# 48 tokens of the last-but-one gathered tile moved behind the last u rows, and the left-hand SBUF buffers set 32 bytes lower, in a GLA/GatedDeltaNet/PEER layer

## The chip, the cores and the metric

The kernel runs on one core of one Trainium2 chip. The metric is the device time of one execution in microseconds (us). The kernel before takes 3274.96 us, the median of three runs between 3272.29 and 3275.75 us.

## What is computed

One layer for 1,024 new frames and 32 sample frames of width 1,024: a mixer of two recurrent heads, then PEER, then a norm. The change lies in PEER, which gives every frame 128 experts (8 heads with 16 each) out of 16,384:

```
act = gelu(einsum('thkd,td->thk', peer_u[eidx], x))
out = einsum('thk,thkd->td', gate * act, peer_v[eidx])
x = x + out ; y = rms_norm(x) * norm_final_w
```

## The kernel before

The frames lie in tiles of 128 tokens, 0 to 7, and "S" with the 32 sample frames. Two ways are used for PEER.

**Dense tiles** (2, 3, 4, 5). All 16,384 experts are computed, in 128 blocks of 128 experts. `activations(blk)` loads a block of u as `ux` (512 KB), splits it into a rounded part and a rest (`uh`, `ul`), and makes `pD` with 24 matmuls of 128x512: 8 slices of the width, each three times (`mm3`: `hh` with `uh`, `hh` with `ul`, `hl` with `uh`; lines 197 to 199). ScalarE makes the Gelu (`w`), VectorE multiplies with the gates `G`, and `w` is split into `wh`, `wl`. The block of v (`vx`, 512 KB) becomes `vh`, `vl`. Four blocks together give `pV` (8 groups of 12 matmuls of 128x512), which VectorE adds to `acc` (L1039). In such a matmul the first operand after the arrow of a row (`hh`, `hl`, `vh`, `vl`) streams through the array, and the second (`uh`, `ul`, `wh`, `wl`) is loaded as its weights. At the end `final_norm` scales each `acc` (L1052) and it is stored.

**Gathered tiles** (0, 1, S, 6, 7, in this order). `u_phase` gathers for each of 128 slots one row of u per token (`ug`, 128x1024, 512 KB, an indirect DMA that GpSimd issues, L1098), and VectorE multiplies and sums it with the token (L1099). `v_phase` gathers for each of 128 tokens its 128 rows of v (L1133); after four tokens TensorE multiplies them with the weights `wd` (eight matmuls of 32x512, L1139, called a round here; 32 rounds for a tile), and the next tokens follow. At the tile's end `pv` is added to the residual `xf`, which is normed and stored; `xf`, the norm's junk and the norm's weights take three of the five `vg` buffers.

`v_phase(t, more)` has five buffers `vg`. With `more` it may also take the four buffers `ug` of the u rows (three in one pool, one in another): token i then uses buffer i mod 9. Up to this version `more` is True for the last tile alone. A tile's v phase is woven with the u phase of the next tile, one gather of each in turn, and the v side is issued at high priority. A scheduler orders the instructions of each engine by its own timing model when the kernel is built; on the chip each engine runs its list in that order.

The order is written out at the end of the kernel: `dense(late)` first, then the loop over the gathered tiles. The scheduler mixes the two, so that TensorE has dense matmuls between the rounds.

SBUF is filled from two sides. On the left lie, among others, the constants (`ident`, `iota128`, `offs`, `firsts`, `noffs`), `c1` to `c3` (later `acc`), the projection's `hh`, `hl`, `wh`, `wl`, and in the dense part `ux`, `vx`, `uh`, `ul`, `G`. On the right lie the dense part's `hh`, `hl`, `w`, `wh`, `wl`, `vh`, `vl`, and `ug`, `vg`, `wd`.

Of the kernel before, what the change touches and what calls it, by code (L numbers as in the profile page):

```python
# [11 lines left out]
F32 = mybir.dt.float32  # L12
# [3 lines left out]
U16 = mybir.dt.uint16  # L16
BF16 = mybir.dt.bfloat16
AF = mybir.ActivationFunctionType
ALU = mybir.AluOpType
AX = mybir.AxisListType  # L20

P = 128
# [10 lines left out]
OFFS = [0, 16, 24, 29, 33, 36, 38, 40, 42, 43, 44, 45, 46, 47, 48, 49]  # L33

PROJ = [[0, 1, "S"], [2, 3, 4], [5, 6, 7]]
GROUPS = [[0], [1, "S"], [2, 3], [4, 5], [6, 7]]

DENSE = [2, 3, 4, 5]
# [20 lines left out]
VB = 5  # L59
NG = NT + 1 - len(DENSE)  # L60
WDB = 3
EARLY = [0, 1, "S"]

SP0 = 2
# [5 lines left out]
def bc(ap, shape):  # L70
    return ap.to_broadcast(shape)
# [3 lines left out]
def layer_kernel(ctx: ExitStack, tc: tile.TileContext, A: dict):  # L75
    nc = tc.nc
    mm = nc.tensor.matmul

    const = ctx.enter_context(tc.tile_pool(name="const", bufs=1))
# [20 lines left out]
    def mixer_tables():  # L100

        tc.keep_in_program_order(nc.scalar.preload_act_table_set("natural_log_exp_and_others"))
# [18 lines left out]
    nc.gpsimd.iota(iota128, pattern=[[1, P]], base=0, channel_multiplier=0,  # L121
                   allow_small_or_imprecise_dtypes=True)

    offs = const.tile([P, 15], F32, name="offs")
    for q in range(15):
        nc.gpsimd.memset(offs[:, q:q + 1], float(OFFS[q + 1]))
    firsts = const.tile([P, 16], U16, name="firsts")
    for q in range(16):
        nc.gpsimd.memset(firsts[:, q:q + 1], OFFS[q] * P)

    noffs = const.tile([P, 15], F32, name="noffs")
    nc.vector.tensor_scalar(noffs, offs, -1.0, 1.0, op0=ALU.mult, op1=ALU.add)

    def row_bcast(name, src, n, pool):
        t = pool.tile([P, n], F32, name=name)
# [3 lines left out]
    def ntok(t):  # L139
        return DEC if t == "S" else P  # L140
# [913 lines left out]
    def idx_of(ap):  # L1054
        return bass.IndirectOffsetOnAxis(ap=ap, axis=0)
# [28 lines left out]
    def u_phase(t, ei, eiT, gate):  # L1084

        act = gs.tile([P, P], F32, name="act", bufs=2)
        h2 = ge.tile([P, D], F32, name="h2", bufs=1)
        slots = DEC if t == "S" else P
        if t == "S":
            for c in range(4):  # L1090
                nc.sync.dma_start(h2[c * DEC:(c + 1) * DEC], h2d[t])
        else:
            nc.sync.dma_start(h2, h2d[t])
        yield None
        for k in range(slots):
            e = t == 0 or k % 4 < 3
            g = (ge if e else gp).tile([P, D], F32, name="ug", bufs=UB if e else 1)
            nc.gpsimd.indirect_dma_start(out=g, out_offset=None, in_=A["u"], in_offset=idx_of(ei[:, k:k + 1]))  # L1098
            nc.vector.scalar_tensor_tensor(g, g, 1.0, h2, op0=ALU.mult, op1=ALU.mult,  # L1099
                                           accum_out=act[:, k:k + 1])  # L1100
            yield None
        with tc.high_priority():
            nc.scalar.activation(act[:, :slots], act[:, :slots], AF.Gelu_apprx_tanh)
            if t in EARLY:
                mixer_tables()
            nc.vector.tensor_tensor(act[:, :slots], act[:, :slots], gate[:, :slots], op=ALU.mult)
            wT = gs.tile([P, P], F32, name="wT", bufs=2)
            pw = bank("pw", "pv")
            by_slot(pw, act, t)
            nc.scalar.copy(wT[:, :ntok(t)], pw[:, :ntok(t)])  # L1110
        ready[t] = eiT, wT

    def v_phase(t, more):

        eiT, wT = ready[t]
        pv = [bank("pv0", "pv"), bank("pv1", "pv")]

        ns = ntok(t) // 4
        W4 = wT[:, :ntok(t)].rearrange("p (c r) -> p c r", c=4)
        for r in range(ns):  # L1120
            wd = gp.tile([P, 4, 32], F32, name="wd", bufs=WDB)
            nc.vector.scalar_tensor_tensor(wd, bc(iota128[:, None, :32], [P, 4, 32]), float(r),
                                           bc(W4[:, :, r:r + 1], [P, 4, 32]), op0=ALU.is_equal, op1=ALU.mult)
            vs = []
            for c in range(4):
                tok = c * ns + r

                own = (r * 4 + c) % (VB + UB + 1)
                if more and own >= VB:
                    g = (ge if own < VB + UB else gp).tile([P, D], F32, name="ug", bufs=UB if own < VB + UB else 1)  # L1130
                else:
                    g = gp.tile([P, D], F32, name="vg", bufs=VB)
                nc.gpsimd.indirect_dma_start(out=g, out_offset=None, in_=A["v"],  # L1133
                                             in_offset=idx_of(eiT[:, tok:tok + 1]))
                vs.append(g)
                yield None

            def product(half, c):
                return mm(pv[half][c * 32:(c + 1) * 32, :], wd[:, c, :], vs[c][:, half * 512:(half + 1) * 512],  # L1139
                          start=(r == 0), stop=(r == ns - 1), tile_position=(0, c * 32), skip_group_check=True)  # L1140

            with tc.issue_after(product(0, 3).ins):
                for half in range(2):
                    for c in range(3 + half):
                        product(half, c)
        x = gp.tile([P, D], F32, name="xf", tag="vg", bufs=VB)
        if t == "S":
            nc.gpsimd.memset(x, 0.0)
            for c in range(4):
                nc.sync.dma_start(x[c * 32:c * 32 + ns], xdram[t][c * ns:(c + 1) * ns])  # L1150
        else:
            nc.sync.dma_start(x, xdram[t])
        for half in range(2):
            cs = slice(half * 512, (half + 1) * 512)
            nc.vector.tensor_tensor(x[:, cs], x[:, cs], pv[half], op=ALU.add)
        nf = gp.tile([P, D], F32, name="nf", tag="vg", bufs=VB)
        load_nfin(nf)
        final_norm(x, gp, nf)
        if t == "S":
            for c in range(4):  # L1160
                nc.sync.dma_start(A["ys"][c * ns:(c + 1) * ns], x[c * 32:c * 32 + ns])
        else:
            nc.sync.dma_start(A["yp"][t * P:(t + 1) * P, :], x)
# [8 lines left out]
    def some(gen, n, pace=1):  # L1172

        while n is None or n > 0:
            for _ in range(pace):
                if next(gen, 0) == 0:
                    return
            n = n and n - 1
            yield None

    def values(t, more):
        return urgent(v_phase(t, more))

    def weave(*gens):
        gens = [g for g in gens if g is not None]
        while gens:
            for g in list(gens):
                if next(g, 0) == 0:
                    gens.remove(g)
# [44 lines left out]
    sel, picked, mixT = {}, {}, {}  # L1234
# [54 lines left out]
    gctx.close()  # L1289
    dv = ctx.enter_context(tc.tile_pool(name="dv", bufs=1, side="right", reuse_waits="tile"))  # L1290
    dense(late)
    prev = None
    for t in [t for g in GROUPS for t in g if t not in DENSE]:
        weave(values(prev, False) if prev is not None else None, u_phase(t, *sel[t]))
        prev = t
    weave(values(prev, True))


OUTS = dict(yp=(SEQ, D), ys=(DEC, D), o_gla_p=(4, 64, 128), o_gdn_p=(4, 128, 128), o_conv_p=(128, 12, 3),
# [62 lines left out]
```

## Time and profile before

| | |
|---|---|
| median of three runs | 3274.96 us (3272.29 to 3275.75) |
| the profiled execution: its own time | 3281.99 us |
| its span, first to last instruction | 3280.3 us |
| TensorE (PE) busy | 3064.6 us, 93% of the span |
| VectorE, GpSimd, ScalarE busy | 2291.9, 1316.8, 1282.0 us |
| moved by DMA | 959.04 MB, mean 292 GB/s |
| mean granted clock of TensorE | 0.961 |

The profile is of one execution. A view by stretches gives each engine's busy time between two times; a timeline lists instructions with what ended the idle time before them. Matmuls are pipelined: one row's duration is longer than the distance between two starts, and the distance is what a matmul costs.

### The profile page before, as it was taken

The page shows a single profiled execution, that of the slowest core. Times are in us where ns is not written, and L with a number is a line of the kernel's source. Part 1 is how long each engine was busy: PE and PEld are TensorE (multiplying, and loading weights), DVE is VectorE, ACT ScalarE, POOL GpSimd, SP SyncE. Part 2 cuts the span into 40 slices and gives each one's busy share as a digit, 9 for nine tenths or more (in the row PEclk, how much of TensorE's full clock was granted, in tenths as well). Part 3 has the DMA queues.
Part 4 walks back from the last instruction along what each step waited for, and adds up shares of the span by engine and source line. Part 5 has one row for each costly group of instructions (what it writes and reads, how often), then busy time and mean ns, then how long its engine had stood idle before and what let it go on. Part 6 is the DMA issues. An engine that isn't in the chain of part 4 may idle for free.

```text
span 3280.3 us, 49506 instructions
## 1 busy us (share of the span) xinstructions
PE 3064.6 (93%) x17739; PEld 2451.9 (75%) x17739; DVE 2291.9 (70%) x5692; ACT 1282.0 (39%) x2748; POOL 1316.8 (40%) x1181
## 2 busy tenths in 40 slices
PE   6999997799999999889789999999999999999997
PEld 6889986689878877767567777777777777776664
DVE  4457478888878989899977767766766767434332
ACT  6758434544332226787523222223222222223111
POOL 2100004433244544433355545544555555233454
PEclk9989998799999989899799999999999999999998
DMA  5532468888788889999999889889998898777988
GB/s 155 167 108 90 155 195 299 271 296 294 272 309 317 310 322 348 314 345 334 328 351 333 336 319 363 329 324 356 334 337 346 300 366 312 281 258 258 339 320 301
DMA packets 363977, 959.04 MB, mean 292 GB/s; under 512 B 35746, under 2 KB 137523, under 8 KB 359635
## 3 DMA queue, kind: packets, MB, share of 16 engines
q0 software_dynamic: 156672, 570.49, 47.5%
q1 hardware_dynamic: 141266, 351.84, 30.5%
q10 hardware_dynamic: 65792, 33.56, 3.5%
q8 instruction: 139, 2.28, 0.3%
q14 instruction: 108, 0.88, 0.1%
HBM read 893.00 MB, written 62.76 MB: 291 GB/s over the span
## 4 chain that ended last, share of the span: by engine, by line
PE 47%; DMA 1%; issue 1%; DVE 1%; POOL 0%; ACT 0%; POOLq 0%; DVEq 0%; ACTq 0%
PE pD L198 7%; PE pD L197 7%; PE pD L199 7%; PE pV L197 7%; PE pV L199 7%; PE pV L198 7%; PE pv L1139 6%; DMA vg<-v,eiT 1%; DMA ug<-u,ei 0%; POOL ug L1098 0%; DVE ug L1099 0%; DVE c L887 0%; DVE vl L192 0%; POOL ug L1133 0%; DVE xf L1052 0%
## 5 line engine op out<-in xcount | busy, mean ns | idle before, releaser
L1098 POOL DMA_INDIRECT ug<-u,ei x544 | 647.2, 1190 | 1148.8 <-DVE ug L1099 514.0
L1133 POOL DMA_INDIRECT vg<-v,eiT x488 | 582.9, 1194 | 625.8 <-PE pv L1139 453.2
L1099 DVE SCALAR_TENSOR_TENSOR ug<-ug,h 128x1024 f32<-128x1024 f32 x544 | 659.9, 1220 | 106.4 <-DMA ug<-u,ei 104.0
L197 PE MATMUL pD<-hh,uh 128*128 128x512 f32 x1024 | 408.6, 399 | 4.3 <-ACT uh L191 4.2
L198 PE MATMUL pD<-hh,ul 128*128 128x512 f32 x1024 | 408.6, 399 | 3.3 <-DVE ul L192 3.3
L199 PE MATMUL pD<-hl,uh 128*128 128x512 f32 x1024 | 407.4, 398 | 0.0
L198 PE MATMUL pV<-vh,wl 128*128 128x512 f32 x1024 | 401.4, 393 | 0.0
L199 PE MATMUL pV<-vl,wh 128*128 128x512 f32 x1024 | 400.0, 393 | 0.0
L197 PE MATMUL pV<-vh,wh 128*128 128x512 f32 x1024 | 381.5, 395 | 5.0 <-DVE acc L1039 4.3
L1039 DVE TENSOR_TENSOR acc<-acc,pV 128x512 f32<-128x512 f32 x248 | 164.0, 684 | 239.1 <-PE pV L199 213.0
L191 ACT CAST vh<-vx 128x1024 fp32r<-128x1024 f32 x128 | 129.2, 1047 | 509.9 <-PE pV L198 420.0
L991 ACT ACTIVATE w<-pD 128x512 f32<-128x512 f32 x128 | 76.5, 598 | 541.0 <-PE pD L199 482.3
L1139 PE MATMUL pv<-vg,wd 128*32 128x512 f32 x1952 | 267.6, 619 | 17.2 <-DMA vg<-v,eiT 16.4
L192 DVE TENSOR_TENSOR wl<-w,wh 128x512 fp32r<-128x512 f32 x302 | 207.3, 688 | 100.5 <-ACT wh L191 70.3
L191 ACT CAST wh<-w 128x512 fp32r<-128x512 f32 x302 | 186.0, 619 | 185.1 <-PE pcm L324 61.7
L534 PE MATMUL pq<-h2T,wqb 128*128 128x256 f32 (+2 forms) x1280 | 249.0, 348 | 3.5 <-ACT sc L556 2.0
L197 PEld LDWEIGHTS pD<-hh,uh 128*128 128x128 f32 x1024 | 193.4, 189 | 65.6 <-issue 14.1
L197 PEld LDWEIGHTS pV<-vh,wh 128*128 128x128 f32 x1024 | 192.3, 188 | 66.9 <-issue 14.2
L198 PEld LDWEIGHTS pD<-hh,ul 128*128 128x128 f32 x1024 | 193.3, 189 | 64.9 <-issue 12.2
L199 PEld LDWEIGHTS pD<-hl,uh 128*128 128x128 f32 x1024 | 193.2, 189 | 56.7 <-issue 11.7
L199 PEld LDWEIGHTS pV<-vl,wh 128*128 128x128 f32 x1024 | 192.7, 188 | 55.1 <-issue 14.3
L534 PEld LDWEIGHTS pq<-h2T,wqb 128*128 128x128 f32 x1280 | 211.2, 194 | 25.9 <-issue 3.0
(334 smaller groups left out, 5457.9 us busy)
## 6 DMA issues: line engine op xcount, KB each, us to landing
ux<-ut SPq DMA_DIRECT2D x128, 512.0 KB
vx<-v SPq DMA_DIRECT2D x128, 512.0 KB
wqb<-wq SPq DMA_DIRECT2D x80, 576.0 KB
gd<-gst ACTq DMA_DIRECT2D x16, 2048.0 KB
G<-gd SPq DMA_DIRECT2D x32, 1024.0 KB
w<-win_c SPq DMA_DIRECT2D x96, 256.0 KB
wch<-wout SPq DMA_DIRECT2D x40, 512.0 KB
w<-win_t SPq DMA_DIRECT2D x72, 256.0 KB
```

What stands on the lines that cost most here:

```text
L191: nc.scalar.copy(hi, x)
L192: nc.vector.tensor_tensor(lo, x, hi.bitcast(F32), op=ALU.subtract)
L197: mm(out, a[0], b[0], start=first, stop=False, **kw)
L198: mm(out, a[1], b[0], start=False, stop=False, **kw)
L199: mm(out, a[0], b[1], start=False, stop=last, **kw)
L534: mm(p[:, :N], w[:, kb, :], h2T[:, kb, :], start=(kb == 0), stop=(kb == KB - 1))
L991: nc.scalar.activation(w, pD, AF.Gelu_apprx_tanh)
L1039: nc.vector.tensor_tensor(acc[ti][:, cs], before[:, cs], p, op=ALU.add)
L1098: nc.gpsimd.indirect_dma_start(out=g, out_offset=None, in_=A["u"], in_offset=idx_of(ei[:, k:k + 1]))
L1099: nc.vector.scalar_tensor_tensor(g, g, 1.0, h2, op0=ALU.mult, op1=ALU.mult, accum_out=act[:, k:k + 1])
L1133: nc.gpsimd.indirect_dma_start(out=g, out_offset=None, in_=A["v"], in_offset=idx_of(eiT[:, tok:tok + 1]))
L1139: return mm(pv[half][c * 32:(c + 1) * 32, :], wd[:, c, :], vs[c][:, half * 512:(half + 1) * 512], start=(r == 0), stop=(r == ns - 1), tile ...
```

## The change

The weave of the last tile's u phase with tile 6's v phase takes only 80 of tile 6's 128 tokens (`SHARE`). Then `more` is set to True, a list that `v_phase` reads token by token, and the other 48 tokens of tile 6 follow, with all nine buffers. Then comes tile 7's v phase as before. Separately, `offs` is dropped, `noffs` is written directly, and `firsts` has 64 bytes where it had 32.

```diff
+SHARE = 80
-    offs = const.tile([P, 15], F32, name="offs")
-    for q in range(15):
-        nc.gpsimd.memset(offs[:, q:q + 1], float(OFFS[q + 1]))
-    firsts = const.tile([P, 16], U16, name="firsts")
+    firsts = const.tile([P, 32], U16, name="firsts")[:, :16]
     noffs = const.tile([P, 15], F32, name="noffs")
-    nc.vector.tensor_scalar(noffs, offs, -1.0, 1.0, op0=ALU.mult, op1=ALU.add)
+    for q in range(15):
+        nc.gpsimd.memset(noffs[:, q:q + 1], float(1 - OFFS[q + 1]))
...
-                if more and own >= VB:
+                if more[0] and own >= VB:
...
-    prev = None
-    for t in [t for g in GROUPS for t in g if t not in DENSE]:
-        weave(values(prev, False) if prev is not None else None, u_phase(t, *sel[t]))
-        prev = t
-    weave(values(prev, True))
+    gathered, more, sums = [t for g in GROUPS for t in g if t not in DENSE], [False], None
+    for t in gathered:
+
+        weave(some(sums, SHARE) if sums and t == gathered[-1] else sums, u_phase(t, *sel[t]))
+        if t == gathered[-1]:
+            more[0] = True
+            weave(sums)
+        sums = values(t, more)
+    weave(sums)
```

**Where buffers lie.** From `noffs` on, every buffer on the left starts 32 bytes lower in its partition; the right side stays. First bytes, and their remainders by 512 (a matmul's operands start at multiples of 512 bytes from there):

| matmul | streamed operand | weights, before | weights, after |
|---|---|---|---|
| `pD` | `hh` 150304 (288), `hl` 133920 (288) | `uh` 51008 (320), `ul` 59200 (320) | `uh` 50976 (288), `ul` 59168 (288) |
| `pV` | `vh` 100960 (96), `vl` 117344 (96) | `wh` 84576 (96), `wl` 92768 (96) | the same |
| `pcm` (projection) | `hh` 155616 (480) | `wh` 181856 (96) | `hh` and `wh` both 32 lower (448, 64) |

**Order on GpSimd** (`ug<-u` is a u row, `vg<-v` and `ug<-v` are v rows in a v buffer or in a u buffer). The list of the kernel before from tile 7's last u rows on:

```order
L1098 DMA ug<-u,ei 128x1024 x3
L1133 DMA ug<-v,eiT 128x1024
L1133 DMA vg<-v,eiT 128x1024 x4
L1133 DMA ug<-v,eiT 128x1024 x3
L1133 DMA vg<-v,eiT 128x1024 x65
L1133 DMA ug<-v,eiT 128x1024 x4
L1133 DMA vg<-v,eiT 128x1024 x5
```

The same place with the change (its line numbers are one lower):

```order
L1097 DMA ug<-u,ei 128x1024 x3
L1132 DMA ug<-v,eiT 128x1024
L1132 DMA vg<-v,eiT 128x1024 x4
L1132 DMA ug<-v,eiT 128x1024 x3
L1132 DMA vg<-v,eiT 128x1024 x12
L1132 DMA ug<-v,eiT 128x1024
L1132 DMA vg<-v,eiT 128x1024 x5
L1132 DMA ug<-v,eiT 128x1024 x4
L1132 DMA vg<-v,eiT 128x1024 x5
```

Before, the first four v rows in u buffers belong to tile 7, and 65 v rows in the five `vg` follow; now the four belong to tile 6, and its last 48 tokens alternate between both kinds, as tile 7's did and do. The u rows stand where they stood.

**Order on TensorE**, the end of the list before (`pv_28049` and `pv_28050` are the two halves of `pv`):

```order
L199 MATMUL pV<-vl,wh 128x512
L1139 MATMUL pv_28049<-vg,wd 32x512
L1139 MATMUL pv_28049<-ug,wd 32x512
L1139 MATMUL pv_28049<-vg,wd 32x512 x2
L1139 MATMUL pv_28050<-ug,wd 32x512
L1139 MATMUL pv_28050<-vg,wd 32x512 x3
L1139 MATMUL pv_28049<-ug,wd 32x512
L1139 MATMUL pv_28049<-vg,wd 32x512 x2
L1139 MATMUL pv_28049<-ug,wd 32x512
L1139 MATMUL pv_28050<-vg,wd 32x512 x2
L1139 MATMUL pv_28050<-ug,wd 32x512 x2
```

The last round with the change, and what follows it:

```order
L1138 MATMUL pv_28047<-vg,wd 32x512
L1138 MATMUL pv_28047<-ug,wd 32x512 x2
L1138 MATMUL pv_28047<-vg,wd 32x512
L1138 MATMUL pv_28048<-ug,wd 32x512 x2
L1138 MATMUL pv_28048<-vg,wd 32x512 x2
L196 MATMUL pD<-hh,uh 128x512
L197 MATMUL pD<-hh,ul 128x512
L198 MATMUL pD<-hl,uh 128x512
```

Before, three rounds stand last with nothing between them (the third is left out here); now 113 dense matmuls stand behind the last round, 21 of `pD` and 92 of `pV`. From tile 6's 21st round on both lists hold 44 rounds and 1,391 dense matmuls. Between the last round of tile 6 and the first of tile 7 stand 55 dense matmuls before and 92 now; between tile 6's 20th and 21st round 47 before and 40 now, and its 22nd follows the 21st at once.

**Order on ScalarE** with the change, near its end (the norm of tile 7's `xf`, then the last Gelu):

```order
L190 CAST wh<-w 128x512
L166 ACTIVATE rs_junk,rs_ss<-xf 128x1024
L171 ACT_TABLE_LOAD
L171 ACTIVATE rs_r<-rs_ss,eps 128x1
L172 ACT_TABLE_LOAD
L172 ACTIVATE rs_r<-rs_r 128x1
L990 ACT_TABLE_LOAD
L990 ACTIVATE w<-pD 128x512
L104 ACT_TABLE_LOAD
L190 CAST wh<-w 128x512
```

Before, the last Gelu had one table load behind it and none ahead, and that norm stood at the list's end.

## Rows read from the trace of the kernel before

**Rows 1.** The page: span, and busy time of each engine.

```profile
span 3280.3 us, 49506 instructions
PE 3064.6 (93%) x17739; PEld 2451.9 (75%) x17739; DVE 2291.9 (70%) x5692; ACT 1282.0 (39%) x2748; POOL 1316.8 (40%) x1181
```

**Rows 2.** By stretches: length, busy us (instructions) of PE, PEld, DVE, ACT, POOL; clock, DMA, GB/s.

```profile
2900.00:3000.00 100.00, 100.00 (x489) 71.62 (x482) 41.28 (x54) 24.42 (x32) 29.39 (x29) 1.00 0.73 258
3000.00:3100.00 100.00, 98.19 (x494) 66.02 (x493) 40.69 (x57) 28.10 (x37) 41.20 (x42) 1.00 0.85 310
3100.00:3150.00 50.00, 50.00 (x261) 32.71 (x260) 18.99 (x27) 10.15 (x13) 24.10 (x24) 1.00 0.89 334
3250.00:3281.00 31.00, 11.91 (x64) 3.21 (x56) 4.93 (x6) 3.29 (x8) 7.05 (x7) 0.69 0.61 230
```

**Rows 3.** Timeline of PE, its last rows (start, us; idle before and its releaser).

```profile
3252.46 0.40 PE L199 MATMUL pV<-vl,wh 128*128 128x512 f32 x1
...
3260.16 1.03 PE L1139 MATMUL pv<-ug,wd 128*32 128x512 f32 x1 [4.82 <-DMA ug<-v,eiT]
...
3269.09 1.03 PE L1139 MATMUL pv<-vg,wd 128*32 128x512 f32 x1 [5.29 <-DMA vg<-v,eiT]
...
3271.67 0.90 PE L1139 MATMUL pv<-vg,wd 128*32 128x512 f32 x1
```

**Rows 4.** By stretches, within the last rounds.

```profile
3260.00:3265.00 5.00, 3.64 (x16) 0.68 (x16) 0.00 (x0) 0.00 (x0) 0.00 (x0) 0.50 1.01 385
```

**Rows 5.** Timeline of PE around tile 6's last rounds and tile 7's first.

```profile
2855.05 1.92 PE L1139 MATMUL pv<-vg,wd 128*32 128x512 f32 x16
...
3023.84 0.40 PE L197 MATMUL pD<-hh,uh 128*128 128x512 f32 x1
3026.05 1.07 PE L1139 MATMUL pv<-vg,wd 128*32 128x512 f32 x8 [1.81 <-DMA vg<-v,eiT]
```

**Rows 6.** Timeline of GpSimd: issues of v rows around those rounds.

```profile
2848.21 0.94 POOL L1133 DMA_INDIRECT vg<-v,eiT  x1 [0.31 <-issue]
...
3017.86 1.67 POOL L1133 DMA_INDIRECT vg<-v,eiT  x1 [2.98 <-DVE xf L1052]
...
3021.84 0.97 POOL L1133 DMA_INDIRECT vg<-v,eiT  x1 [2.31 <-DMA yp<-xf]
```

**Rows 7.** Timeline of DVE at the end: the last dense sum, its norm, tile 7's norm.

```profile
3252.89 0.69 DVE L1039 TENSOR_TENSOR acc<-acc,pV 128x512 f32<-128x512 f32 x1 [1.66 <-PE pV L199]
3255.36 1.28 DVE L1052 SCALAR_TENSOR_TENSOR acc<-acc,rs_r,nfD 128x1024 f32<-128x1024 f32 x1 [1.78 <-ACT rs_r L173]
...
3275.12 1.29 DVE L1052 SCALAR_TENSOR_TENSOR xf<-xf,rs_r,nf 128x1024 f32<-128x1024 f32 x1 [1.78 <-ACT rs_r L173]
```

**Rows 8.** Groups of ScalarE from 1600 us on: table loads (count, busy us, mean ns).

```profile
L991 ACT ACT_TABLE_LOAD x6 | 7.7, 1283 | 0.1
```

**Rows 9.** Timeline of PE: first and last of 34 `pD`, of 23 `pV` back to back.

```profile
3003.92 0.39 PE L198 MATMUL pV<-vh,wl 128*128 128x512 f32 x1
...
3008.91 0.39 PE L199 MATMUL pV<-vl,wh 128*128 128x512 f32 x1
...
3016.14 0.39 PE L197 MATMUL pD<-hh,uh 128*128 128x512 f32 x1
```

**Rows 10.** Timeline of PE in the projection: 20 `pcm` of 384 columns between these.

```profile
248.82 0.87 PE L324 MATMUL pcm<-hl,wh 128*128 128x384 f32 x4
...
252.34 0.33 PE L754 MATMUL pi<-T,XT 128*128 128x64 f32 x2
```

**Rows 11.** Groups of PE: count, busy us, mean ns, idle before.

```profile
L199 PE MATMUL pD<-hl,uh 128*128 128x512 f32 x1024 | 407.4, 398 | 0.0
L199 PE MATMUL pV<-vl,wh 128*128 128x512 f32 x1024 | 400.0, 393 | 0.0
```

**Rows 12.** Groups of DVE from 1600 us on, the same columns.

```profile
L192 DVE TENSOR_TENSOR ul<-ux,uh 128x1024 fp32r<-128x1024 f32 x128 | 156.6, 1224 | 16.0 <-ACT uh L191 14.3 <-issue 1.5
L192 DVE TENSOR_TENSOR vl<-vx,vh 128x1024 fp32r<-128x1024 f32 x128 | 154.3, 1219 | 37.4 <-ACT vh L191 28.6 <-issue 8.8
```

## The prediction

> **What bounds the kernel now.** I read the page first: PE is busy for 93% of the span and no other engine comes near [rows 1]. A mean over stages decides nothing, so the view by stretches came next. From about 1800 us on PE is busy practically all the time at the full clock, up to 3250 us: 100 of 100, 98.2 of 100, 50 of 50 us. Only in the last 31 us is it busy for 11.9 [rows 2]. So TensorE bounds the stage in which the change lies, and the reader should see what follows: gathering rows faster is worth nothing there by itself. It pays only where PE waits for a row.
>
> The timeline shows these places. The last dense matmul starts at 3252.46. Then PE waits 4.82 us for a v row, works, waits 5.29 us for another, and its last row begins at 3271.67 [rows 3]. [...] A second wait, of 1.81 us, lies between tile 6 and tile 7 at 3026.05 [rows 5].
>
> Why the rows are late shows on GpSimd. With five buffers four rows are in flight per round: the last row for the round that starts at 2855.05 is issued at 2848.21, 6.8 us earlier [rows 5, 6]. In that stage DMA moves only 258 GB/s, and 29 gathers are issued per 100 us. With nine buffers it is 334 GB/s and 24 per 50 us, and PE still is busy 50 of 50 us [rows 2]. So the kernel spends tile 6's last part with slow gathers and much dense work between rounds, and then lacks dense work at the end.
>
> **The change, part by part.**
>
> *The 48 tokens.* The instructions are the same: 44 rounds and 1,391 dense matmuls from tile 6's 21st round on, as many gathers, as many bytes. What moves is the dense work between the rounds: 113 dense matmuls now stand behind the last round, none before. A round is 1.92 us [rows 5]. The three last rounds now cost the stretch from 3252.86 (the end of the last dense row) to 3272.57 (the end of the last row) [rows 3], 19.7 us, where three rounds at the full clock cost 5.8. Gain: 13.9 us.
>
> The 1.81 us between the tiles: there 55 dense matmuls of about 0.23 us (12.7 us) lie between the rounds, so tile 6's last round ended at about 3011.4. Tile 7's first rows are late because `xf`, junk and norm weights hold three `vg` buffers: issues at 3017.86, after the norm, and at 3021.84, after the store was done [rows 6]. The first was there at 3026.05, 8.2 us after its issue; so the second should be there at about 3030, 18.6 us after tile 6 ends. 92 dense matmuls now cover 21 us. Gain: 1.8 us. Together 15.7.
>
> *What comes instead at the end.* The chain is then the last `pV`, the sum, the norm, the store. The same chain is in the trace: from the end of the last dense matmul at 3252.86 to the end of the scaling at 3256.64 it takes 3.8 us; for tile 7 from 3272.57 to 3276.41, also 3.8 [rows 3, 7]. The store is the same 512 KB. So nothing is lost there. One thing is new ahead of it: the last Gelu waits on ScalarE behind tile 7's norm and three table loads of 1.28 us each [rows 8], a fourth follows. From the last round's end that is about 2 us of sums on VectorE, 1.2 for the square, 5.1 for the loads and some 2.5 for the small operations, the Gelu and the cast, 11 us. PE has 21 `pD` and 31 `pV` that don't need it, 12 us. I cost it at nothing; if that cover fails it is 1 or 2 us.
>
> *New waits inside.* Rows of the 21st and 22nd round share five `vg` buffers with the 20th; 40 dense matmuls (9.2 us) stand between, where 6.8 us from the last issue, plus about 4 us for four issues, sufficed with 47. Bounds: nothing, or 2 us. I take nothing, since half of those rows come into buffers that are free long before.
>
> *The 32 bytes: VectorE, ScalarE, DMA.* `ul` is made from operands on the left alone, `vl` mostly from the right, and the two sides differ by 32 in the remainder by 64: 1224 and 1219 ns [rows 12]. I cost this at nothing. `noffs` loses one VectorE instruction in the first microseconds, where VectorE waits for the input anyway.
>
> *The 32 bytes: TensorE.* Here the rows show something odd. 34 starts of `pD` in a row lie 7.70 us / 33 = 233.3 ns apart, 23 of `pV` 4.99 / 22 = 226.8 ns [rows 5, 9], though both are 128x512 with new weights for each. On the whole the groups' means differ by 5 ns [rows 11]. What differs is the place of the operands. In `pV` streamed operand and weights have the same remainder by 512 (96 and 96), in `pD` not (288 and 320). `pcm` has unequal ones too (480 and 96), and its 384 columns take 3.52 / 20 = 176.0 ns [rows 10], where 384/512 of `pV`'s distance would be 170.1: again 6 ns more. With the change `pD`'s are equal (288 and 288). If the inequality is the cause, `pD` comes down to `pV`: at most 6.5 ns x 3,072 = 20.0 us, by the groups' means 5 x 3,072 = 15.4. If it is not the cause, nothing. `pcm` keeps its distance. Since PE is the bound in nearly all of the dense stage, a gain there is a gain of the kernel. Three rows of one pattern speak for it and none against; I take 16.
>
> [...]
>
> **The sum.** 13.9 + 1.8 + 16.0 = 31.7 us. Against the profiled execution that is 3281.99 - 31.7 = 3250.3 us; that one lay 7.0 us above the median, so the median should be 3274.96 - 31.7 = 3243.3 us.
>
> **The rivals.**
>
> *The shift does nothing.* For it: I have only three kinds of matmul, and `pD` differs from `pV` also in its groups' length and its bank. Against it: the same 6 ns in `pcm`, which is in another stage. Then 15.7 us alone: 3259.3.
>
> *The gathers cannot keep up in the new place.* 176 gathers of 0.524 MB and 29 blocks of 1.31 MB (two loads and a quarter of `G`) are 130 MB from the 21st round on; PE needs 1,391 x 0.23 + 44 x 1.92 = 404 us for the matmuls: 322 GB/s. 334 were moved with PE full [rows 2]. So this needs stalls in single rounds: 0.36 us in each of 44 would eat the 15.7. With no gain on `pD` that is no change, 3275.
>
> *The weights' new place costs more instead.* Where equal remainders made the two reads meet more often, `pD` would slow down. It decides from 15.7 + 6.5 = 22.2 us on, 7.2 ns for each of 3,072, a distance of 240.5 ns; at 245 ns it is 36 us, less 15.7: 3295. Against it: `pV` has equal remainders and is the fastest; no row above lies over 233.3.
>
> **How the numbers follow.** The measurement tells about 0.2% (6.5 us) from no change. Both gains: 0.50. The shift does nothing: 0.32. Late gathers: 0.07, no change. Dearer weights: 0.06, slower. Another 0.05 for a gain beyond the first case, for instance in the projection, whose buffers now start at multiples of 64. So faster 0.87, same 0.07, slower 0.06. The likeliest is 3243; its own range, from a gain on `pD` of 8 to 20 us with 2 to 4 us more or less of waits, is 3235 to 3253. To hold 8 in 10 the range must reach over the second case, with up to 4 us of new stalls: 3232 to 3264.
>
> **What would show it right or wrong.** The sum over rounds: PE has no gap over 1 us after its last round, its clock stays at 1.00 until the end, and the last rows are `pV`, a sum, a norm and a store of `acc`. The wait between tiles 6 and 7 is gone. GpSimd issues tile 6's last 48 rows at about the pace of tile 7's, and DMA moves over 300 GB/s where it moved 258. `pD` starts lie 227 ns apart, not 233; `pV` stays at 227. Wrong would make it: `pD` still at 233 (then 3259), several rounds waiting for a row, or ScalarE's last Gelu late, with PE idle ahead of the last `pV`.

## The result, and the profile after

The changed kernel takes 3236.55 us, the median of six runs (3229.78 to 3253.13), where the kernel before took 3273.62 us beside it (3267.14 to 3282.03): a ratio of 0.9896 with an interval of 0.9871 to 0.9921, 37 us by the medians. The forecast was 3243.3 us, and as a ratio 3243.3 / 3274.96 = 0.9903. A second measurement on another chip gave 0.9928 (0.9901 to 0.9956), 3226.95 against 3246.08 us. On its own, the kernel before has medians from 3246 to 3274 us on the chips met here. That is as much as the change is worth, so times are compared below only as ratios to the kernel before on the same chip. The two intervals of the change overlap; by them its gain lies between 0.4% and 1.3%. Stretches of profiles are compared across chips; where PE is full they agree (the last column of the table below has 451.3 and 451.1 us for the change on two chips).

The page of the changed kernel, span and busy time:

```profile
span 3237.2 us, 49507 instructions
PE 3036.7 (94%) x17739; PEld 2443.9 (75%) x17739; DVE 2288.8 (71%) x5691; ACT 1284.7 (40%) x2751; POOL 1311.8 (41%) x1181
```

The view by stretches (columns as in [rows 2]), with the last one from shortly before the last round to the last matmul:

```profile
2900.00:3000.00 100.00, 99.61 (x509) 68.72 (x509) 40.51 (x57) 26.36 (x36) 38.46 (x40) 1.00 0.88 326
3000.00:3100.00 100.00, 99.99 (x522) 65.72 (x521) 38.69 (x54) 24.42 (x32) 50.22 (x49) 1.00 0.94 351
3199.00:3230.00 31.00, 30.53 (x142) 23.52 (x140) 13.82 (x18) 13.88 (x24) 0.00 (x0) 1.00 0.17 68
```

Where DMA moved 258 GB/s between 2900 and 3000 us it now moves 326, with 40 GpSimd issues where there were 29, and PE is still full. At the end PE is busy for 30.53 of 31 us at a clock of 1.00; before, it was busy for 11.91 of 31 at 0.69 [rows 2].

The timeline of PE at the end (start, us; an idle time before a row would stand behind it):

```profile
3203.05 0.59 PE L1138 MATMUL pv<-vg,wd 128*32 128x512 f32 x1
3203.57 0.49 PE L196 MATMUL pD<-hh,uh 128*128 128x512 f32 x1
...
3229.14 0.39 PE L198 MATMUL pV<-vl,wh 128*128 128x512 f32 x1
```

The last round is followed at once by the 113 dense matmuls, with no wait. The waits of 4.82 and 5.29 us of [rows 3] have no counterpart, and the wait of 1.81 us between tiles 6 and 7 [rows 5] is gone as well: from 2860 us on only one wait over 0.2 us is left, of 0.39 us. Ahead of that lie a wait of 1.08 us before tile 6's 20th round, where the kernel before has 0.51, and one of 0.57 us before its 24th; before the 21st and 22nd, of which the prediction was unsure, there is none.

On ScalarE the last Gelu and the cast behind it, with the table loads that the order put there:

```profile
3209.14 1.28 ACT L990 ACT_TABLE_LOAD   x1
3210.43 0.60 ACT L990 ACTIVATE w<-pD 128x512 f32<-128x512 f32 x1
3211.05 1.28 ACT L104 ACT_TABLE_LOAD   x1
3212.34 0.62 ACT L190 CAST wh<-w 128x512 fp32r<-128x512 f32 x1
```

The cast ends 9.9 us after the last round's last start, and PE had `pV` of earlier blocks to do meanwhile.

A run of 32 `pD` without a break, behind a round:

```profile
3185.39 0.40 PE L198 MATMUL pD<-hl,uh 128*128 128x512 f32 x1
...
3187.72 0.39 PE L196 MATMUL pD<-hh,uh 128*128 128x512 f32 x1
...
3192.48 0.39 PE L196 MATMUL pD<-hh,uh 128*128 128x512 f32 x1
```

From the first to the eleventh start it is 2.33 us / 10 = 233 ns, the distance of [rows 5]. From there the other 21 take 4.76 / 21 = 226.7 ns, the distance of `pV` in [rows 9]. So `pD` reaches the shorter distance, but behind a round only after some ten matmuls: over its 33 runs of more than twenty behind a round the first ten distances average 231.7 ns and the next ten 226.7, where in 26 such runs of the kernel before they average 233.0 and 233.3. `pV` behind a round does as `pD` does now, before the change (231.8 and 226.7) and after it (231.3 and 226.7), which is why the means lie above 226.7: over all distances between 200 and 260 ns, `pD` has a mean of 233.3 before and 228.1 now, `pV` 228.2 and 228.5.

**Where the time went, by stretches.** For every kernel below four points of its trace are used: the first dense matmul, the 600th, the 4,600th (counted from zero; the order of all engines up to there is the same in all of them, but for the constants at the start and for `share_56`, which has one round more in its last stretch), and the start of PE's last matmul.

| kernel | to the first dense | to the 600th | 600th to 4,600th | 4,600th to PE's last | ratio to before (interval) |
|---|---|---|---|---|---|
| before | 1603.0 | 168.5 | 1030.6 | 469.6 | 1 |
| `shift_alone` | 1577.8 | 166.4 | 1023.6 | 469.6 | 0.9958 (0.9939 to 0.9978) |
| `order_alone` | 1576.9 | 166.4 | 1030.2 | 453.4 | 0.9945 (0.9927 to 0.9964) |
| `pad_back` | 1578.4 | 166.4 | 1027.1 | 454.0 | 0.9941 (0.9920 to 0.9961) |
| the change | 1592.9 | 166.6 | 1018.3 | 451.3 | 0.9896 (0.9871 to 0.9921) |
| the change (`change_again`) | 1567.6 | 166.7 | 1020.4 | 451.1 | 0.9928 (0.9901 to 0.9956) |
| `pad_192` | 1576.0 | 168.6 | 1023.0 | 451.7 | one run |
| `share_104` | 1570.4 | 166.5 | 1021.1 | 455.5 | 0.9905 (0.9876 to 0.9933) |
| `share_56` | 1583.2 | 167.0 | 1021.8 | 455.6 | 0.9920 (0.9892 to 0.9948) |
| `share_120` | 1577.7 | 167.0 | 1018.8 | 461.2 | 0.9941 (0.9918 to 0.9965) |
| `wh_64` | 1575.5 | 166.9 | 1022.8 | 451.3 | 0.9889 (0.9854 to 0.9924) |
| `wh_64_again` | 1564.0 | 166.2 | 1022.1 | 450.6 | 0.9880 (0.9853 to 0.9907) |

The two profiled executions differ by 43.1 us of span, more than the medians. Of that, 10.1 us lie in the first column, which varies from 1564.0 to 1603.0 us among kernels that don't differ in that part's order. The two highest, 1603.0 and 1592.9, are from the first measurement, beside which the kernel before took 3274 us; in the later ones it took 3246 to 3253. The largest single piece of the 10.1 us is a late store of the gates. PE in the kernel before, and at the same place after:

```profile
1353.18 1.65 PE L959 MATMUL pgm<-gB,gA 128*128 128x128 f32 x6 [7.98 <-ACT gA L956]
```

```profile
1347.78 1.65 PE L958 MATMUL pgm<-gB,gA 128*128 128x128 f32 x6 [2.19 <-ACT gA L955]
```

ScalarE in the kernel before waited for the store of `gst`:

```profile
1350.34 0.58 ACT L960 COPY gst<-pgm 128x512 f32<-128x512 f32 x1 [5.68 <-DMA gd<-gst]
```

Nothing of the change lies there, and the 10.1 us are left out of all that follows.

### The profile page after: what moved, and what is told of

It is laid out like the page before. It is cut to its first block, busy times and chain, and to the rows that moved or that the text cites. A ratio compares the mean times of both kernels' runs of the same rounds, so it can differ in the third digit from the quotient of the medians.

```text
span 3237.2 us, 49507 instructions
## 1 busy us (share of the span) xinstructions
PE 3036.7 (94%) x17739; PEld 2443.9 (75%) x17739; DVE 2288.8 (71%) x5691; ACT 1284.7 (40%) x2751; POOL 1311.8 (41%) x1181
## 4 chain that ended last, share of the span: by engine, by line
PE 45%; issue 2%; DMA 2%; DVE 2%; POOL 1%; ACT 0%; DVEq 0%; SPq 0%; POOLq 0%
PE pV L196 7%; PE pV L197 7%; PE pV L198 7%; PE pD L197 6%; PE pD L198 6%; PE pD L196 6%; PE pv L1138 5%; DMA ug<-v,eiT 1%; DMA vg<-v,eiT 1%; DVE ug L1098 0%; POOL vg L1132 0%; DMA ug<-u,ei 0%; POOL ug L1097 0%; DMA yp<-xf 0%; DVE vl L191 0%
## 5 line engine op out<-in xcount | busy, mean ns | idle before, releaser
L1132 POOL DMA_INDIRECT vg<-v,eiT x467 | 556.2, 1191 | 507.3 <-PE pv L1138 347.2
L1098 DVE SCALAR_TENSOR_TENSOR ug<-ug,h 128x1024 f32<-128x1024 f32 x544 | 660.1, 1219 | 112.0 <-DMA ug<-u,ei 109.9
L1138 PE MATMUL pv<-vg,wd 128*32 128x512 f32 x1868 | 257.5, 608 | 7.3 <-DMA vg<-v,eiT 6.4
L197 PEld LDWEIGHTS pV<-vh,wl 128*128 128x128 f32 x1024 | 192.8, 188 | 53.4 <-issue 12.6
```

Source lines behind the costliest of these rows:

```text
L197: mm(out, a[1], b[0], start=False, stop=False, **kw)
```

## The experiments

**The two parts apart.** `order_alone` has the new order and the constants of the kernel before; `shift_alone` the constants of the change and the order of the kernel before.

```diff
 # order_alone, against the change
-    firsts = const.tile([P, 32], U16, name="firsts")[:, :16]
+    offs = const.tile([P, 15], F32, name="offs")
...
+    firsts = const.tile([P, 16], U16, name="firsts")
...
+    nc.vector.tensor_scalar(noffs, offs, -1.0, 1.0, op0=ALU.mult, op1=ALU.add)
```

> The order alone: SHARE and the nine buffers for tile 6's last 48 tokens, all buffers where they lay before (weights of pD at 320, streamed operand at 288). My theory (two gains that add up, the order 15.7 us and the place of the operands 16 us): some 15.7 us below the kernel before, about 3258 us where that one takes 3274; pD starts 233 ns apart as before; last round followed by dense matmuls, no PE gap over 1 us at the end. Rival 1 (the order is the whole gain): as fast as the changed kernel, about 3237. Rival 2 (the place of the operands is the whole gain): as slow as before, 3274.

```diff
 # shift_alone, against the kernel before
-    offs = const.tile([P, 15], F32, name="offs")
...
-    firsts = const.tile([P, 16], U16, name="firsts")
+    firsts = const.tile([P, 32], U16, name="firsts")[:, :16]
...
+        nc.gpsimd.memset(noffs[:, q:q + 1], float(1 - OFFS[q + 1]))
```

> The 32 bytes alone: constants as in the change, order of all engines as before. My theory: about 16 us below the kernel before (3258), pD 227 ns from start to start, the waits of 4.8 and 5.3 us at the end and the one between the tiles still there. Rival 1: no gain, 3274, pD at 233. Rival 2 (all of the gain is here): about 3237.

On one chip with the kernel before at 3249.44 us: `order_alone` 3232.00 us, ratio 0.9945, that is 3249.44 x 0.0055 = 17.9 us (11.7 to 23.7); `shift_alone` 3235.97 us, ratio 0.9958, 13.6 us (7.1 to 19.8). So neither part is nothing. That neither is the whole gain the times alone don't show, since both intervals overlap that of the change's second measurement (0.9901 to 0.9956); the traces below show it. The product of the two ratios is 0.9903, between the two of the change. In `order_alone` `pD` stays at the old distance, here 36 distances in 8.40 us, 233.3 ns, while the end is that of the change:

```profile
3126.45 0.39 PE L199 MATMUL pD<-hh,uh 128*128 128x512 f32 x1
...
3134.85 0.40 PE L199 MATMUL pD<-hh,uh 128*128 128x512 f32 x1
```

In `shift_alone` `pD` has a mean distance of 228.0 ns, and the end is that of the kernel before, only worse:

```profile
3217.88 0.40 PE L196 MATMUL pV<-vl,wh 128*128 128x512 f32 x1
3219.43 0.62 PE L1136 MATMUL pv<-vg,wd 128*32 128x512 f32 x1 [1.15 <-DMA vg<-v,eiT]
...
3225.35 0.59 PE L1136 MATMUL pv<-ug,wd 128*32 128x512 f32 x1 [3.99 <-DMA ug<-v,eiT]
...
3234.82 1.03 PE L1136 MATMUL pv<-vg,wd 128*32 128x512 f32 x1 [7.07 <-DMA vg<-v,eiT]
```

The three waits sum to 12.21 us where they were 0.55, 4.82 and 5.29 before, and the one between the tiles is 2.48 for 1.81. The table has the consequence: its last stretch is 469.6 us, as before. What the faster `pD` gained behind the 4,600th dense matmul (759 of them by 5.2 ns, some 3.9 us) was given back whole: PE's idle time there grew from 13.0 to 16.1 us, all of it for rows. With the new order the same shift gains there: 453.4 and 454.0 without, 451.3 and 451.1 with.

**Is it `uh` and `ul`, or another buffer?** `pad_back` is the change with 32 unused bytes ahead of the dense part's left buffers.

```diff
     da = ctx.enter_context(tc.tile_pool(name="da", bufs=1, reuse_waits="tile"))
+    da.tile([P, 8], F32, name="pad")
```

> The changed kernel with 32 unused bytes ahead of the dense part's buffers on the left (ux, vx, uh, ul, G): these lie where they lay before, all other buffers on the left stay 32 bytes lower. The order of all engines is that of the change. My theory (only uh and ul against hh and hl matter): pD back at 233 ns, the time that of the order alone, about 3258. Rival (the shift works somewhere else, in the projection, the router or in DMA): the time of the changed kernel, about 3237.

3234.38 us, ratio 0.9941, close to the 0.9945 of `order_alone`, though its interval overlaps that of the change's second measurement. The distance of `pD` decides it:

```profile
3125.40 0.39 PE L196 MATMUL pD<-hh,uh 128*128 128x512 f32 x1
...
3133.80 0.40 PE L196 MATMUL pD<-hh,uh 128*128 128x512 f32 x1
```

These 36 distances take 8.40 us, 233.3 ns each, though all other buffers on the left lay as in the change. So the 32 bytes act through this pool. That it is `uh` and `ul` in it, and not `ux` or `G`, follows from the next kernel, where nothing but matmuls runs.

**How the distance depends on the two places.** `map` computes none of the layer.

```diff
+    for s in "abc":
+        for w in weights.values():
+            group(streams[s], w, 512, 48)
+    for cols in (384, 256):
+        for w in weights.values():
+            p = group(streams["a"], w, cols, 48)
```

> None of the layer is computed: only matmuls of constants with 128 weight columns, in groups of 48, nothing else on the chip. First 4 groups to begin with, then 48 groups of 512 columns: streamed operand sa, sb, sc (first byte 128, 160, 192 by 512), each with weights wA to wP (first byte 224, 256, ... in steps of 32, 16 places that cover 512 bytes); then 16 groups of 384 and 16 of 256 columns with sa. Theory A (the relation of the two places sets the distance): about 227 ns where both have the same remainder (sa with wN, sb with wO, sc with wP), about 233 at the others or at some of them, and the fast place moves by one letter with the streamed operand. Theory B (the weights' own place counts): the same letters are fast with sa, sb and sc. Theory C (it needs other engines or DMA beside it): all 48 groups alike.

The timeline of PE; a row is a group of 48 matmuls, so the difference of two starts by 48 is the distance:

```profile
108.75 11.05 PE L99 MATMUL p<-sa,wF 128*128 128x512 f32 x48
119.64 11.35 PE L99 MATMUL p<-sa,wG 128*128 128x512 f32 x48
130.83 0.40 PE L99 MATMUL p<-sa,wH 128*128 128x512 f32 x1
...
175.62 11.16 PE L99 MATMUL p<-sa,wL 128*128 128x512 f32 x48
186.62 11.36 PE L99 MATMUL p<-sa,wM 128*128 128x512 f32 x48
197.81 11.05 PE L99 MATMUL p<-sa,wN 128*128 128x512 f32 x48
208.70 11.35 PE L99 MATMUL p<-sa,wO 128*128 128x512 f32 x48
219.89 11.36 PE L99 MATMUL p<-sa,wP 128*128 128x512 f32 x48
...
375.95 11.36 PE L99 MATMUL p<-sb,wN 128*128 128x512 f32 x48
387.14 11.05 PE L99 MATMUL p<-sb,wO 128*128 128x512 f32 x48
398.03 11.35 PE L99 MATMUL p<-sb,wP 128*128 128x512 f32 x48
409.22 11.35 PE L99 MATMUL p<-sc,wA 128*128 128x512 f32 x48
```

With `sa`, `wN` takes 10.89 / 48 = 226.9 ns and `wO` 11.19 / 48 = 233.1. With `sb`, which lies 32 bytes higher, `wO` is the fast one (10.89) and `wN` not (11.19). So it is the relation of the two places, theory A, and neither a place as such nor something that other engines must add. One thing differs from the theory: `wF` and `wG`, 256 bytes below by the remainders, take the same 10.89 and 11.19 as `wN` and `wO`, so the pattern repeats after 256 bytes, not 512. By weights less streamed, modulo 256 (mean distances in ns, without the first five of each group):

| | 0 | 32 | 64 | 96 | 128 | 160 | 192 | 224 |
|---|---|---|---|---|---|---|---|---|
| 512 columns | 226.7 | 233.3 | 233.3 | 234.3 | 232.4 | 233.3 | 228.9 | 233.3 |
| 384 columns | 173.3 | 173.3 | 174.6 | 176.7 | 176.1 | 176.7 | 173.3 | 176.6 |
| 256 columns | 119.9 | 118.4 | 117.8 | 118.0 | 118.6 | 120.0 | 117.8 | 117.8 |

Which place is fast depends on the number of streamed columns. With 384 a distance of 32 bytes costs nothing (173.3 ns at both), and with 256 equal places are among the slowest (119.9):

```profile
750.33 5.91 PE L99 MATMUL p<-sa,wF 128*128 128x256 f32 x48
756.08 5.84 PE L99 MATMUL p<-sa,wG 128*128 128x256 f32 x48
761.75 5.82 PE L99 MATMUL p<-sa,wH 128*128 128x256 f32 x48
767.41 5.79 PE L99 MATMUL p<-sa,wI 128*128 128x256 f32 x48
```

Here `wF` with equal places takes 5.75 / 48 = 119.8 ns, `wH` 64 bytes on 5.66 / 48 = 117.9. (The 118.0 at 96 is the mean of two groups that differ, 118.7 and 117.3.)

The cases of the kernel before stand in the table: `pD` at 32 (233.3 in its trace), `pV` at 0 (226.8), `pcm` at 128 (176.0).

**Does the map hold inside the kernel?** `pad_192` is `pad_back` with 192 bytes in place of 32.

> The changed kernel with 192 unused bytes ahead of the dense part's buffers on the left, so that the weights of pD lie 192 above the streamed operand (64 below it by 256). If the map holds inside the kernel, pD takes 228.9 ns, between 226.7 and 233.3, and pV stays at 226.7; the time is some 3,072 x 2.2 ns = 7 us above the changed kernel. If nearness of the two places were what counts, or equality by 512, pD would be at 233.

A run of 37 `pD`:

```profile
3119.28 0.39 PE L196 MATMUL pD<-hh,uh 128*128 128x512 f32 x1
...
3127.53 0.40 PE L196 MATMUL pD<-hh,uh 128*128 128x512 f32 x1
```

8.25 / 36 = 229.2 ns, and 229.6 over all, where the map has 228.9: neither nearness nor equality alone describes it. Its one run, 3229.01 us, decides nothing, and neither does its middle stretch as it stands: 1023.0 lies within the 1018.3 to 1023.6 of the kernels with equal places. Less PE's idle time and the time that the lower clock withheld (the length by one minus the mean granted clock, an estimate from the trace), the stretch is 1018.1 us; `order_alone` and `pad_back` have 1024.6 and 1024.3 by the same working, the two profiles of the change 1015.0 and 1014.6. So it lies between the two placings, as the map has it.

**What collides with what.** `pairs` computes none of the layer either. It alternates two pairs of operands, and varies the number of weight columns, the banks and the type.

```diff
+    group(["Na", "Ob"], 512, 96)
+    group(["Oa", "Nb"], 512, 96)
+    group(["Na"], 512, 48, banks=2)
...
+    group(["Na"], 512, 48, same=True)
...
+    for rows in (64, 32):
+        for w in "FGHIJKLM":
+            group([w + "a"], 512, 48, rows=rows)
```

> None of the layer is computed: only matmuls of constants. Streamed sa lies at 128, sb at 160 by 256; weights wF and wN at 128, wG and wO at 160, wH at 192, and so on in steps of 32. After 192 matmuls to begin with: wN with sa (equal places) 226.7 ns and wO with sa (32 apart) 233.3 as in the map; then 96 that alternate wN,sa and wO,sb (each pair equal, but the weights of the next lie 32 from what streams now), then 96 that alternate wO,sa and wN,sb (each pair 32 apart, the next weights equal to what streams now). Theory A1 (the next matmul's weights are loaded while this one streams, and these two reads collide): the first alternation takes 233, the second 226.7. Theory A2 (what counts is the pair of one matmul): the first 226.7, the second 233. Then each of the two pairs with two PSUM banks in turn (A1 and A2: no change; a bank's own cost would show as less than 226.7), and with the same 128 weight columns every time (no change, if they are loaded anew). Then 64 and 32 weight columns with eight places each: if the load's read collides, the spread over the places, 7.6 ns with 128 columns, falls to about 4 and 2. Then fp32 in place of fp32r, 256 columns and 128 weight columns, and 512 columns with 32 weight columns (the form of a round): no forecast, since no row shows it; a spread of some ns in the same places if every load collides alike.

The first alternation took 231.9 ns, the second 230.1: neither A1 nor A2, and neither is the fast 226.7. Two banks and unchanged weights changed nothing (226.7 and 233.4, 226.7 and 233.3). With 64 weight columns the eight places lie from 228.4 to 232.7, a spread of 4.3 as expected, but with 32 columns from 230.4 to 240.0, where 2 was expected; a load's read that collides in proportion to its columns is not the whole story, and no theory here gives the numbers. Nor do equal places have the shortest distance there: with 64 weight columns they take 230 ns, and 192 bytes has the 228.4:

```profile
163.41 11.20 PE L104 MATMUL p<-sa,wF 128*64 128x512 f32 x48
174.45 11.28 PE L104 MATMUL p<-sa,wG 128*64 128x512 f32 x48
...
229.97 11.13 PE L104 MATMUL p<-sa,wL 128*64 128x512 f32 x48
240.94 11.24 PE L104 MATMUL p<-sa,wM 128*64 128x512 f32 x48
```

With 32 they take 231.7. With fp32 all eight places are alike. An fp32 matmul leaves two rows in the trace (as the eight matmuls of a round leave 16), and these lie 215.8 ns apart for 256 columns with 128 weight columns and 429.2 for 512 with 32, so a matmul takes twice that. In the kernel before, rows of `pq`, of fp32 with 256 columns and 128 weight columns as well, lie 216.0 ns apart (the mean of 701 distances).

**How many tokens must go?** `share_104`, `share_56` and `share_120` change that number alone.

```diff
-SHARE = 80
+SHARE = 104
```

> SHARE 104 in place of 80: only tile 6's last 24 tokens use nine buffers, and 53 dense matmuls stand behind the last round (113 in the change). The gain on pD stays, 16 us. My theory (the gain of the order is the dense work that is kept for the end): 53 x 0.23 = 12 us of it, so most of the wait at the end is covered; 2 to 8 us above the changed kernel. Rival (any dense work behind the last round is enough): no difference. Rival (nothing but 48 tokens suffice): some 14 us above.

> SHARE 56: the last 72 tokens use nine buffers, 185 dense matmuls stand behind the last round. My theory (TensorE is already full to its last matmul, so more dense work behind adds nothing): the changed kernel's time within 0.2%. Rival (more tokens with nine buffers, more gain): another 3 us or more for each 24 tokens. Rival on the other side: with dense work taken from between the rounds, 24 more tokens wait for their rows, some us slower.

> SHARE 120: tile 6's last 8 tokens use nine buffers; no dense matmul stands behind the last round, as in the kernel before; the 32 bytes as in the change. My theory (the gain of the order is the dense work behind the last round, not the buffers as such): the waits at the end are back, the stretch from the 4,600th dense matmul to the last matmul takes 465 to 470 us as in the kernel with the shift alone (469.6; 451.3 in the change), and the time is 14 to 20 us above the changed kernel. Rival (nine buffers for a few tokens are enough): within 5 us of it.

`share_104` takes 0.9905 of the kernel before, no slower than the change as far as this can tell; its last stretch is 455.5 us, 4.2 longer than the change's, within the 2 to 8 us expected. But not for the reason expected: at the end PE waits for nothing, and the longer waits lie earlier, 2.04 us before tile 6's 29th round and 0.89 us within tile 7, both for rows in u buffers. The first of them:

```profile
2903.84 0.62 PE L1138 MATMUL pv<-ug,wd 128*32 128x512 f32 x1 [2.04 <-DMA ug<-v,eiT]
```

So dense work for the end was not short with 53 matmuls.

`share_56` takes 0.9920, and its last stretch is 453.7 us without the additional round: TensorE was full already, and the two waits left in that stretch, 1.02 and 1.42 us, are for `vl` and `uh` and not for rows.

`share_120` went against the expectation: 461.2 us, 9.9 above the change and not 14 to 19, and its median was 2.7 us above the change's beside it, within the 5 us of the rival, with overlapping intervals (0.9941 and 0.9928). The end of its PE:

```profile
3213.77 0.39 PE L198 MATMUL pV<-vl,wh 128*128 128x512 f32 x1
...
3222.15 1.03 PE L1138 MATMUL pv<-vg,wd 128*32 128x512 f32 x1 [6.14 <-DMA vg<-v,eiT]
```

One late row is left of two: nine dense matmuls now lie between the last round but one and the one before it, where none lay, though none lies behind the last. So dense work behind the last round is not the only form of the cure, and eight tokens already bring part of it.

**The projection by the map.** `pcm` lies at 128, a slow place, and the map has faster ones. In `wh_64` its weights lie 64 below the streamed operand; `ptm`, where the roles are exchanged, is then at 64.

```diff
-            ss = p1.tile([P, 1], F32, name="ss", bufs=2)
+            ss = p1.tile([P, 16], F32, name="ss", bufs=2)[:, :1]
```

> The changed kernel with the projection's weights 64 bytes higher (ss 64 bytes wide in place of 4): wh and wl lie at 128 by 256, hh and hl at 192, so weights 64 below in pcm and 64 above in ptm. By the map's groups of 384 and 256 columns: pcm 176.1 to 173.3 ns, ptm 118.7 to 117.8. With 1,224 pcm and 1,296 ptm that is 3.4 and 1.2 us, if TensorE sets the projection's pace; the time is then 0 to 5 us below the changed kernel, which this measurement hardly tells from nothing. Rival (the map doesn't hold in the projection, where other engines and DMA use SBUF): pcm stays at 176.

> The changed kernel as it is, on the chip of the two beside it, so that both are compared with it there. 3,222 to 3,232 us where the kernel before takes some 3,255 (ratio 0.990).

Four groups of four `pcm` in the change, and in `wh_64`:

```profile
246.86 0.87 PE L323 MATMUL pcm<-hl,wh 128*128 128x384 f32 x4
...
249.68 0.87 PE L323 MATMUL pcm<-hh,wl 128*128 128x384 f32 x4
```

```profile
247.98 0.86 PE L323 MATMUL pcm<-hl,wh 128*128 128x384 f32 x4
...
250.75 0.85 PE L323 MATMUL pcm<-hh,wl 128*128 128x384 f32 x4
```

2.82 / 16 = 176.3 ns became 2.77 / 16 = 173.1 (over all 176.0 and 173.4); `ptm` went from 118.0 to 115.2, more than the map's groups of 256 columns had. The time was 3215.36 us where the change took 3226.95 beside it, ratios 0.9889 and 0.9928.

> The kernel of wh_64 once more, since its ratio (0.9889) lay lower than its two shorter distances account for: 1,224 pcm x 2.6 ns + 1,296 ptm x 2.8 ns = 6.8 us at most, that is 0.002 below the change (0.9896 and 0.9928 in two measurements). If that is all, 0.988 to 0.991; if the first measurement was right as it stood, 0.989 or less; if the projection gains nothing, 0.991 or more.

3211.94 us, ratio 0.9880 (0.9853 to 0.9907) on yet another chip. Both ratios of this version lie below both of the change, with overlapping intervals, so the times don't show a gain; the distances account for 6.8 us or 0.002 at most. The traces show something in the projection itself: its last `ptm` starts at 816.5 and 814.7 us here and between 817.8 and 828.1 in the ten profiles without this edit, 821.0 and 821.3 in those of the change. By the start of the first dense matmul the scatter covers it (1575.5 us here, 1567.6 in the change beside it).

## Why the prediction was right, step by step

*The end and the wait between the tiles, 15.7 us.* The last stretch took 453.4 us with the new order alone against 469.6: 16.2 us, and the part behind the last matmul 8.0 against 8.6. The mechanism is the one forecast: the waits are gone and the clock stays at 1.00. The cover of ScalarE's loads held, and "I take nothing" for new waits held within a microsecond (0.57 and 0.39 us, neither where it was feared). That the dense work has to stand behind the last round was too narrow: `share_120` has none there and still loses only 9.9 us of the 18 between `shift_alone` and the change.

*The gathers in the new place.* 326 to 351 GB/s with PE full; the rival of late gathers, which needed 0.36 us in each of 44 rounds, fell.

*The 32 bytes, 16 us.* The step that rested on three rows of one pattern was right in kind: equal remainders bring `pD` to `pV`'s distance. As a rate it was right in size as well: 233.3 to 228.1 ns is 5.2 x 3,072 = 16.0 us. But not all of it became time. Between the 600th and the 4,600th dense matmul `order_alone`, `pad_back` and the kernel before average 1029.3 us; the seven profiles with equal places and the same matmuls there run from 1018.3 to 1023.6 and average 1021.0: 8.3 us, and 9.9 by the two profiles of the change alone. In the last stretch it is 2.5. Ahead of the 600th there is nothing to see (166.4 without, 166.6 with): PE there waits for `ul` (3.3 us before, 2.5 now) and `acc` (4.3 and 4.2). So the kernel gains some 11 us from it, where 16 was forecast; `shift_alone` measured 13.6 (7.1 to 19.8), which agrees with either. Less idle time and the lower clock, as for `pad_192` above, the three stretches of `order_alone` and `pad_back` are 2.3, 9.6 and 3.2 us longer than those of the change, 15.2 in all: the matmuls did become shorter by nearly what was forecast, and some 4 us of it went into waits and clock. "PE is the bound in nearly all of the dense stage" was the step that was a little too generous; [rows 2] begin at 2900 us, and of the first stretch above PE in the kernel before is idle for 8.4 us, at a mean clock of 0.96.

*The sum.* By the stretches the two parts give 16.2 + 0.6 + 11 = 28 us, less than the 31.7 forecast. The first measurement had 37 us and the second 19, so that the forecast came within 7 us of the first median is in part luck.

*The reading of the remainders.* By 512 was wrong, by 256 is right; here both say the same. That equal places are the one cause was too narrow too: a distance of 192 is nearly as fast. And the row of `pcm` carried less than it seemed to: at 384 columns the fastest place takes 173.3 ns, not the 170.1 scaled from `pV`, so place accounts for 2.7 of the 6 ns. The rule held because `pD` has 512 columns and 128 weight columns; at 256 columns equal places are slow (119.9, where three others have 117.8).

*The rivals.* That the shift does nothing, 0.32, was the serious one, and `shift_alone` and `pad_back` refute it (`pD` has a mean distance of 228.0 ns in the first, 233.3 in a run of the second): the map has 6.6 ns between two places 32 bytes apart, 226.7 and 233.3. The weights' new place was not dearer. The further gain for which 0.05 was kept, in the projection, did not come with this change, since `pcm` keeps its relation, but `wh_64` has its distances.

*VectorE, at nothing:* `ul` and `vl` take 1223 and 1219 ns where they took 1224 and 1219 [rows 12].

Open: why the relation of the two places matters. The map tells when the distance is short, not why, and that two reads disturb one another is a guess that `pairs` did not bear out. That the store of the gates was late by chance in the kernel before is argued from the spread of the first column, not shown. That the change itself makes nothing shorter ahead of the dense stage is not shown either; the scatter there is larger than the 10.1 us.

## What to carry to other kernels

Where TensorE is full with fp32r matmuls, compare the distance of starts of two groups of one shape. If they differ, look at where weights and streamed operand start, modulo 256 bytes: here, with 512 columns and 128 weight columns, equal starts cost 226.7 ns and most others 233, and 32 bytes ahead of one pool decided it. For another shape measure the places anew, since with 256 columns (117.8 ns at 64, 192 and 224 bytes, 119.9 at equal places) or fewer weight columns (with 64, 228.4 at 192 bytes, 230 at equal places) other places had the shortest distance. And keep work that needs no gather for the end of the engine's list: in the last stretch a faster matmul alone only lengthened the wait for the last rows (`shift_alone`: 469.6 us as before, PE idle for 16.1 us where it was 13.0), while with the new order the same stretch became shorter by it (453.4 and 454.0 us without, 451.3 and 451.1 with).

## What the runs showed of the hardware

With nothing else running, the distance of fp32r matmuls with 512 columns and 128 new weight columns goes from 226.7 to 234.3 ns with the relation of the two operands' first bytes, repeating after 256 bytes; which relation is fast changes with the shape (with 256 columns equal places take 119.9 and three others 117.8). fp32 matmuls show no such dependence (rows 215.8 ns apart at all eight places). In the kernel, with equal places, the short distance is not there at once: behind a round the first ten distances of `pD` average 231.7 ns (233 in the run shown), and then the run falls to 226.7 and stays there, while at a distance of 32 bytes a run stays at 233.3 to its end (8.40 us for 36 distances in `order_alone` and in `pad_back`). In the map, where group follows group without a break, the first ten distances of `wF` and `wN` with `sa` are 226.7 already. The clock was lower behind the waits, as before the change (0.50 between 3260 and 3265 us, behind the idle 4.82 us [rows 3, 4]): in `share_120` the granted clock between 3222 and 3225 us is 0.50, behind the idle 6.14 us, where it was 1.00 between 3215 and 3220.
